# The last down block of each layer by seven quarter products, on one Trainium2 core

## The chip, the core and the metric

The kernel runs on one core of one Trainium2 chip. The core has a matrix engine (TensorE, PE in the profile), two elementwise engines (VectorE, DVE; ScalarE, ACT), a general engine (GpSimd, POOL) and a queue engine that issues most transfers (SyncE, SP). Each engine works through its own instructions in order; they wait for each other by semaphores. The results of matmuls land in eight PSUM banks of 128 rows by 512 float32.

The metric is the device time of one execution in microseconds (us), lower is better. Three runs of the kernel before took 1818.7, 1818.74 and 1818.12 us; the median is 1818.7 us.

## What is computed

A decoder trunk of two layers over 512 tokens of width 1024. Only the second half of a layer matters here, the MLP with its two norms:

```python
h2 = rmsnorm(x, pre_mlp_g)
ff = jnp.square(jax.nn.relu(h2 @ w_ff1)) @ w_ff2     # 1024 -> 4096 -> 1024
return x + rmsnorm(ff, post_mlp_g)
```

The output is the (1, 512, 1024) array after the second layer. After the first layer, x is normed again (`pre_mix_g`) and multiplied by the next input projection.

## The kernel before

**Precision.** Every float32 matmul is done as three: both operands are split into a high part (rounded) and a low part (the rest), and hi·hi + hi·lo + lo·hi are added in PSUM. A weight chunk of 128x1024 numbers is loaded by SP (`load`, L278), its high part made by ACT (L384, tile `wh`), its low part by DVE (L385, tile `wl`). `weights()` (L389) hands out the chunks in the fixed order of `chunk_order` (L58) and prepares four ahead (`LOOK = 4`, four `wh` and four `wl` buffers; six `wr` buffers for the raw loads).

**The MLP.** The hidden width 4096 is done in four stages `s` of 1024. Each stage has an up block (h2 times a 1024-wide part of `w_ff1`, relu, square) and a down block (the result times a 1024-row part of `w_ff2`), and the four down blocks are summed. The sums are held in SBUF in `acc[t][n]`, eight 128x512 tiles: token tile `t` of 0 to 3, output half `n` of 0 or 1.

**Up blocks.** `SEQ[s]` (L45) gives the order of the eight 128-wide units of a stage. A plain unit is 24 matmuls of 512 columns (`mm_a`, L396). A pair in brackets, such as `(0, 1)`, is done by seven products of four 128-row blocks instead of eight (Winograd's form of Strassen's scheme): 84 matmuls of 256 columns (`mm_h`, L482), with sums of weights by DVE (L343). Stage 0 is plain, stages 1 and 2 mixed, stage 3 all pairs.

**Down blocks.** Stages 0 to 2 use the same scheme over quarters (512x512 blocks of the 1024x1024 weights, two token halves): seven products P1 to P7, each `mm_c` (L466) with 24 matmuls of 512 columns: 2 chunks `j` by 2 token tiles `t` by 2 row blocks by 3. `seven` (L291) makes the seven right operands from loaded quarters with sums by DVE (L304, L309); `lefts` and `make_later` (L1542, L1557) make the left ones. The order is P1, P5, P6, P2, P7, P3, P4. Each finished quarter is added to `acc` by DVE out of PSUM (`into` L1413, L1614, L1617, L1627). P4 of a stage is cut in two around the first product of the next stage where that starts with a pair (`split4`, L1629).

**Stage 3 before** (L1636 to L1668) is plain in its down block: `acc[t][0]` is copied into PSUM by ACT and 96 matmuls are added to it (`mm_b4`, L448), then mean square and gain for that half; then the other half, token tile by token tile.

- Layer 0 uses `last_tiles` (L427): tile 0 (24 matmuls), tile 1 (24), then tiles 2 and 3 together (48) with the transposes of the finished tiles 0 and 1 between them (`norm_turn`, L554: eight transposes on PE, then split by ACT and DVE into the next layer's left operand). The next layer starts with tiles 0 and 1 (42 matmuls of 432 columns) while tiles 2 and 3 are normed, then turns those.
- Layer 1 does one tile after the other, and writes each out.

**The tail of a token tile** is `post_tiles` (L559): mean square by ACT (L520), times the gain by DVE (L575), a small add (L525), the power by POOL (L526), then two DVE instructions that scale and add x (L578, L579). With a next layer follow the mean square of the new x (ACT, twice), the power again, and two scalings by DVE (L535), which make what the transposes read. Within one call the order of DVE and ACT is written out by hand (`Order`, L179); in the other places a planner in the compiler sets each engine's order before the run, mostly by program order among what it thinks ready.

## Time and profile before

| | us |
|---|---|
| median of 3 runs | 1818.7 |
| the profiled execution's own time | 1816.19 |
| its span, from the first to the last instruction | 1814.5 |
| layer 0, stage 2: P1's first matmul to P4's first | 785.63 to 818.51 |
| layer 0, stage 3 to the next layer's first matmul | 818.51 to 909.72 |
| layer 1, stage 2: P1's first matmul to P4's first | 1684.91 to 1717.79 |
| layer 1, stage 3, to its last matmul | 1717.79 to 1807.04 |

How to read it: the first part of the page gives the busy time of each engine. Rows of the timeline give the start of an instruction, its duration, engine, line, and operands by the program's names; what stands in square brackets is idle time of that engine before it, with what ended it. Matmuls overlap: one of 512 columns is listed with 0.39 us, but the next one starts sooner, so what a row of matmuls costs is read from their starts. The table of windows gives the busy time of each engine in a stretch, with the number of instructions, the granted TensorE clock and the share and rate of the transfers.

### The profile page before, as it was taken

The page shows a single profiled execution, that of the slowest core. Times are in us where ns is not written, and L with a number is a line of the kernel's source. Part 1 is how long each engine was busy: PE and PEld are TensorE (multiplying, and loading weights), DVE is VectorE, ACT ScalarE, POOL GpSimd, SP SyncE. Part 2 cuts the span into 40 slices and gives each one's busy share as a digit, 9 for nine tenths or more (in the row PEclk, how much of TensorE's full clock was granted, in tenths as well). Part 3 has the DMA queues.
Part 4 walks back from the last instruction along what each step waited for, and adds up shares of the span by engine and source line. Part 5 has one row for each costly group of instructions (what it writes and reads, how often), then busy time and mean ns, then how long its engine had stood idle before and what let it go on. Part 6 is the DMA issues. An engine that isn't in the chain of part 4 may idle for free.

```text
span 1814.5 us, 28394 instructions
## 1 busy us (share of the span) xinstructions
PE 1794.6 (99%) x10252; PEld 1524.7 (84%) x10252; DVE 1375.1 (76%) x2590; ACT 1007.5 (56%) x2065; POOL 210.6 (12%) x386
## 2 busy tenths in 40 slices
PE   9999999999999999999999999999999999999998
PEld 8878878888788888989898887888877888889896
DVE  5499796887666878898556997968875669698973
ACT  6678742444434656566556877234443347566572
POOL 0322102221101000000013221022111010000000
PEclk9999999999999999999999999999999999999999
DMA  5633447655463254554445334585545533555551
GB/s 201 203 112 121 111 146 226 178 172 152 117 208 129 82 164 156 174 180 145 168 160 176 106 127 111 169 232 159 163 140 154 171 116 105 174 162 164 174 178 56
DMA packets 146431, 278.60 MB, mean 154 GB/s; under 512 B 33569, under 2 KB 66657, under 8 KB 146290
## 3 DMA queue, kind: packets, MB, share of 16 engines
q1 hardware_dynamic: 145778, 276.75, 49.2%
q8 instruction: 81, 1.33, 0.3%
q14 instruction: 60, 0.49, 0.1%
q0 software_dynamic: 512, 0.03, 0.0%
HBM read 239.38 MB, written 37.36 MB: 153 GB/s over the span
## 4 chain that ended last, share of the span: by engine, by line
PE 88%; DVE 4%; ACT 4%; DMA 2%; issue 1%; POOL 0%; SPq 0%; DVEq 0%; POOLq 0%; ACTq 0%
PE ps_b L459 3%; PE ps_b L461 3%; PE ps_b L463 3%; PE ps_f L400 2%; PE ps_f L401 2%; PE ps_f L402 2%; PE ps_us L400 2%; PE ps_ud L400 2%; PE ps_us L401 2%; PE ps_ud L401 2%; PE ps_ud L402 2%; PE ps_us L402 2%; PE ps_vp L400 2%; PE ps_vp L402 2%; PE ps_vp L401 1%; PE ps_qp L401 1%
## 5 line engine op out<-in xcount | busy, mean ns | idle before, releaser
L384 ACT CAST wh<-wr 128x1024 fp32r<-128x1024 f32 (+2 forms) x368 | 372.7, 1019 | 430.4 <-PE ps_us L401 60.2
L385 DVE TENSOR_TENSOR wl<-wr,wh 128x1024 fp32r<-128x1024 f32 (+2 forms) x368 | 434.9, 1189 | 183.8 <-ACT wh L384 180.2
L526 POOL TENSOR_TENSOR pr<-pq,pw 128x1 f32<-128x1 f32 x16 | 9.8, 615 | 790.1 <-DVE pq L525 790.1
L459 PE MATMUL ps_b<-wh,h_h 128*128 128x432 f32 (+1 forms) x192 | 71.1, 370 | 0.0
L461 PE MATMUL ps_b<-wl,h_h 128*128 128x432 f32 (+1 forms) x192 | 70.4, 367 | 0.0
L463 PE MATMUL ps_b<-wh,h_l 128*128 128x432 f32 (+1 forms) x192 | 70.3, 366 | 0.0
L400 PE MATMUL ps_f<-g_h,wh 128*128 128x512 f32 x160 | 62.4, 390 | 0.0
L401 PE MATMUL ps_f<-g_l,wh 128*128 128x512 f32 x160 | 62.4, 390 | 0.0
L402 PE MATMUL ps_f<-g_h,wl 128*128 128x512 f32 x160 | 62.2, 389 | 0.0
L401 PE MATMUL ps_qp<-h_l,wh 128*128 128x512 f32 x128 | 53.9, 421 | 0.0
L400 PE MATMUL ps_vp<-h_h,wh 128*128 128x512 f32 x128 | 53.7, 420 | 0.0
L402 PE MATMUL ps_vp<-h_h,wl 128*128 128x512 f32 x128 | 53.7, 419 | 0.0
L995 ACT ACTIVATE M<-M,nm 128x128 f32<-128x128 f32 x128 | 49.8, 391 | 5.9 <-DVE nm L990 5.8
L400 PE MATMUL ps_qp<-h_h,wh 128*128 128x512 f32 x128 | 51.8, 405 | 0.0
L343 DVE TENSOR_TENSOR wr<-wr 128x512 f32<-128x512 f32 x72 | 47.5, 685 | 5.5 <-DMA wr<-in_weights_dram 5.2
L400 PE MATMUL ps_kp<-h_h,wh 128*128 128x512 f32 x128 | 51.6, 403 | 0.0
L402 PE MATMUL ps_qp<-h_h,wl 128*128 128x512 f32 x128 | 51.4, 401 | 0.0
L401 PE MATMUL ps_vp<-h_l,wh 128*128 128x512 f32 x128 | 51.3, 401 | 0.0
L401 PE MATMUL ps_ga<-h_l,wh 128*128 128x512 f32 x128 | 51.0, 398 | 0.0
L400 PE MATMUL ps_gb<-h_h,wh 128*128 128x512 f32 x128 | 51.0, 398 | 0.0
L402 PE MATMUL ps_kp<-h_h,wl 128*128 128x512 f32 x128 | 50.9, 398 | 0.0
L402 PE MATMUL ps_ga<-h_h,wl 128*128 128x512 f32 x128 | 50.7, 396 | 0.0
(435 smaller groups left out, 5928.4 us busy)
## 6 DMA issues: line engine op xcount, KB each, us to landing
wr<-in_weights_dram SPq DMA_DIRECT2D x320, 512.0 KB, 3.6
wr<-in_weights_dram SPq DMA_DIRECT2D x24, 432.0 KB, 5.2
D<-dd SPq DMA_DIRECT2D x32, 256.0 KB, 2.7
xd<-xo SPq DMA_DIRECT2D x12, 512.0 KB, 3.0
xt<-xd SPq DMA_DIRECT2D x24, 256.0 KB, 4.5
D<-gd SPq DMA_DIRECT2D x16, 256.0 KB, 6.2
dd<-D SPq DMA_DIRECT2D x16, 256.0 KB, 5.2
kkd<-kk SPq DMA_DIRECT2D x16, 256.0 KB, 2.0
```

The lines of the kernel that those rows point to most:

```text
L343: tt(out=o_, in0=i0, in1=i1, op=ALU.add)
L384: nc.scalar.copy(wh[:, :w], wr[:, :w])
L385: sub(out=wl[:, :w], in0=wr[:, :w], in1=wh[:, :w].bitcast(F32), op=ALU.subtract)
L400: mm(ps, lhsT=wh[:, k, :], rhs=hi, start=k == 0, stop=False)
L401: mm(ps, lhsT=wh[:, k, :], rhs=lo, start=False, stop=False)
L402: mm(ps, lhsT=wl[:, k, :], rhs=hi, start=False, stop=k == KT - 1)
L459: mm(pss[t], lhsT=hi[:, tsl], rhs=wh[:, r, :], start=k == 0 and not onto, stop=False, skip_group_check=onto)
L461: mm(pss[t], lhsT=hi[:, tsl], rhs=wl[:, r, :], start=False, stop=False, skip_group_check=onto)
L463: mm(pss[t], lhsT=lo[:, tsl], rhs=wh[:, r, :], start=False, stop=k == KT - 1, skip_group_check=onto)
L526: ptt(out=r, in0=q1, in1=mhalf[:, 0:1], op=ALU.pow)
L995: act(out=M[:, j * P:(j + 1) * P], in_=M[:, j * P:(j + 1) * P], func=AF.Exp, bias=nm[:, j:j + 1], accum_out=den[:, j:j + 1])
```

## The change

The change makes stage 3 of each layer like stage 0: its up block is plain (`SEQ[3]` becomes `FF_ORDER`), and its down block is done by the seven quarter products. Three things differ from the other stages. The order of the products is P1, P5, P6, P2, P3, P7, P4, with the right operands made in that order. Sums that are held in `acc` are added by DVE into PSUM before the last product of a quarter (`pa`, `pv`, and `pw_` after P7), so that the finished numbers stand in PSUM. Token tiles 0 and 1 are finished after P3 and go through `post_tiles` together, tiles 2 and 3 after P4; there the half that is finished last is half 0 (`late = 0`). In layer 0 the transposes of tiles 0 and 1 stand behind the first and second half of P4. In layer 1 P4 is done for tile 2 and then for tile 3.

```diff
-SEQ = (FF_ORDER, (0, 1, (4, 5), (2, 3), 6, 7), ((0, 1), (4, 5), (2, 3), 6, 7), ((0, 1), (2, 3), (4, 5), (6, 7)))
+SEQ = (FF_ORDER, (0, 1, (4, 5), (2, 3), 6, 7), ((0, 1), (4, 5), (2, 3), 6, 7), FF_ORDER)
@@ chunk_order
             out.append(("up", l, s))
-            if s < 3:
-                out.append(("seven", "w_ff2", l, s * 1024))
-                continue
-            for n in range(2):
-                for j in range(4):
-                    b_in("w_ff2", s * 1024 + j * 256, n * 512, 512)
+            out.append(("seven", "w_ff2", l, s * 1024))
@@ seven
+        if r0 == 3072:
+            makes = makes[:4] + (makes[5], makes[4], makes[6])
@@ mm_c
-    def mm_c(pss, left, onto=False, js=range(2)):
+    def mm_c(pss, left, onto=False, js=range(2), ts_=range(2), ws=None):
         for j in js:
-            wh, wl = weights()
+            wh, wl = ws[j] if ws else weights()
             hi, lo = left[j]
-            for t in range(2):
+            for t in ts_:
@@ post_tiles: 512: and :512 become hb_ and ha, set by the new argument late
+        ha, hb_ = (slice((h_ % 2) * 512, (h_ % 2 + 1) * 512) for h_ in (late + 1, late))
@@ ff2_tail
+            late = 0 if tiles[0] > 1 else 1
+            a0 = [a[1 - late] for a in acc]
@@ the stages
-        for s in range(3):
+        for s in range(4):
...
-                make("P4", T[2], a22, -1.0)
+                make("P4", T[2], a22, -1.0 if s < 3 else 1.0)
...
             make_later("P3", T[1])
+            if s == 3:
+                break
@@ stage 3, in place of ff1, mm_b4, last_tiles and the loop over tiles
+        def early_half(t, n, src):
+            s0[t] = meansq(src, "pq0")
+            tt(out=acc[t][n], in0=src, in1=gb3[:, n * 512:(n + 1) * 512], op=ALU.mult)
+
+        for t in range(2):
+            tt(out=pa[t], in0=pa[t], in1=acc[t][0], op=ALU.add)
+            tt(out=pv[t], in0=pv[t], in1=acc[t][1], op=ALU.add)
         if l < depth - 1:
             nxt = pre_begin(l + 1)
             xs_next = []
+        mm_c(pa, left["P2"], True)
+        for t in range(2):
+            early_half(t, 0, pa[t])
+        mm_c(pv, left["P3"], True)
+        ff2_tail((0, 1), pv)
+        mm_c(pw_, left["P7"], True)
+        for t in range(2):
+            tt(out=acc[2 + t][1], in0=pw_[t], in1=acc[2 + t][1], op=ALU.add)
+            tt(out=pw_[t], in0=acc[2 + t][0], in1=pw_[t], op=ALU.subtract)
+        for t in range(2):
+            early_half(2 + t, 1, acc[2 + t][1])
+        if l < depth - 1:
             order = Order(nc.tensor)
             order.begin()
-            last_tiles(ws, h3, "ps_f2", ff2_tail, lambda t: norm_turn(xs_next[t], t, nxt[1]),
-                       [a[1] for a in acc])
+            for j in range(2):
+                mm_c(pw_, left["P4"], True, (j,))
+                norm_turn(xs_next[j], j, nxt[1])
+            ff2_tail((2, 3), pw_)
             hT = nxt
         else:
-            for t in range(NT):
-                ps = (PS if t % 2 else PZ)("ps_f2")
-                nc.scalar.copy(ps, acc[t][1])
-                mm_b(ps, ws, h3, t, onto=True)
-                ff2_tail((t,), [ps])
+            ws = [weights() for j in range(2)]
+            for t in range(2):
+                mm_c(pw_, left["P4"], True, ts_=(t,), ws=ws)
+                ff2_tail((2 + t,), pw_[t:])
```

## The prediction

> **What bounds the kernel now.** I read the page's busy times and its chain first, then the timeline of PE around both stages 3, then DVE's groups and timeline in stage 2, which already has the down block that stage 3 is to get.

> ```profile
> span 1814.5 us, 28394 instructions
> ...
> PE 1794.6 (99%) x10252; PEld 1524.7 (84%) x10252; DVE 1375.1 (76%) x2590; ACT 1007.5 (56%) x2065; POOL 210.6 (12%) x386
> ...
> PE 88%; DVE 4%; ACT 4%; DMA 2%; issue 1%; POOL 0%; SPq 0%; DVEq 0%; POOLq 0%; ACTq 0%
> ```

> PE is busy 99% of the span and 88% of the chain: a matmul less is time less, as long as nothing makes PE wait. The timeline of PE gives what a matmul costs and where the stages lie:

> ```profile
> 818.51 0.39 PE L475 MATMUL ps_pw<-wh,P_h 128*128 128x512 f32 x1
> ...
> 821.23 0.28 PE L487 MATMUL ps_a<-g_h,wh 128*128 128x256 f32 x1
> ...
> 822.67 0.40 PE L475 MATMUL ps_pw<-wh,P_h 128*128 128x512 f32 x1
> ...
> 864.83 0.40 PE L463 MATMUL ps_b<-wh,h_l 128*128 128x512 f32 x1
> ...
> 886.16 0.39 PE L420 MATMUL ps_f<-wh,h_h 128*128 128x512 f32 x1
> ...
> 909.72 0.35 PE L420 MATMUL ps_b<-wh,h_h 128*128 128x432 f32 x1
> ```

> From 818.51 to 821.23 stand 12 matmuls of 512 columns: 2.72/12 = 0.2267 us each. From 821.23 to 822.67 stand 12 of 256 columns: 1.44/12 = 0.120 us each. From 818.51 to 909.72 (91.21 us) stand 24 + 192 of the first kind, 336 of the second and 16 transposes (0.79 us per eight, first row of the fence on the transposes below): 5.44 + 43.53 + 40.32 + 1.58 = 90.9. So stage 3 has no gap worth the name, and PE bounds it alone.

> DVE is the engine to look at next. Its windows in stage 2, from P1's first matmul to P4's, in layer 0 and in layer 1:

> ```profile
> 785.63:818.51 32.88, 32.88 (x146) 27.21 (x145) 31.41 (x38) 19.20 (x26) 0.00 (x0) 1.00 0.50 160
> 1684.91:1717.79 32.88, 32.88 (x146) 27.21 (x145) 31.02 (x37) 19.30 (x26) 0.00 (x0) 1.00 0.52 160
> ```

> The third pair is DVE: 31.41 of 32.88 us, 96%. ACT (19.2) and the transfers (share 0.50) have room. The six products there run on a DVE that is nearly full. What it does, by groups, and its first and last steps:

> ```profile
> L385 DVE TENSOR_TENSOR wl<-wr,wh 128x1024 fp32r<-128x1024 f32 x11 | 13.2, 1222 | 2.0 <-ACT wh L384 2.0
> ...
> L304 DVE TENSOR_TENSOR wr<-wr 128x1024 f32<-128x1024 f32 x3 | 3.7, 1223 | 0.2 <-DMA wr<-in_weights_dram 0.2
> L309 DVE TENSOR_TENSOR wr<-wr 128x1024 f32<-128x1024 f32 x2 | 2.4, 1218 | 0.0
> ...
> L1417 DVE TENSOR_TENSOR acc<-ps_pa,acc 128x512 f32<-128x512 f32 x2 | 1.3, 684 | 0.0
> ...
> L1614 DVE TENSOR_TENSOR acc<-ps_pw,acc 128x512 f32<-128x512 f32 x2 | 1.3, 682 | 0.0
> ```

> ```profile
> 786.69 1.22 DVE L385 TENSOR_TENSOR wl<-wr,wh 128x1024 fp32r<-128x1024 f32 x1 [1.78 <-ACT wh L384]
> ...
> 813.39 1.28 DVE L1614 TENSOR_TENSOR acc<-ps_pw,acc 128x512 f32<-128x512 f32 x2
> ```

> DVE starts 1.06 us after P1's first matmul, since it could not work ahead (1.78 us idle: the fourth chunk waits for a buffer that the last up unit still reads), and has its list done at 818.33 (the first L1617, quoted under rival B), just before P4. So there is no spare DVE time in these six products.

> **The change, part by part.** *PE, up block:* 336 matmuls of 256 columns become 192 of 512: 192 x 0.2267 - 336 x 0.120 = 43.53 - 40.32 = +3.21 us per layer. *PE, down block:* 192 become 168: -24 x 0.2267 = -5.44. Net -2.23 per layer, **-4.5 us** in all. [...]

> *Transfers:* the down block loads 16 chunks in place of 8, on SP's queue, ahead of the next layer's. Stage 2 does just that at a share of 0.50, with 0.2 us of DVE waiting for a load; I take nothing. Were that cover gone, one late chunk would cost PE up to its 2.72 us. *ACT* loses the seeds of PSUM and is free. *Up block on DVE:* lighter than before (no L343), but as in stage 2 that buys nothing: the four buffers allow no more to be ahead at P1.

> *DVE in the down block,* until P4 may start. P4 accumulates onto `pw_`, which DVE must first rewrite in place after P7; that wait is new. Stage 2's list stands, minus the four additions out of PSUM behind P2 and P7 (L1417 on `pa`, L1614), plus: four additions into `pa` and `pv`, two multiplications by the gain behind P2, two in the tail of tiles 0 and 1 (L575), the sum for `acc[2][1]` and the rewriting of `pw_[0]`. That is 10 - 4 = 6 instructions of 128x512. An addition that writes PSUM does not occur before; nearest are 0.64 (the pair at 813.39) from below and 0.75 (L578) from above. At 0.62 to 0.64, six are 3.8 us. The tail of tiles 0 and 1 adds, by the groups of layer 0's end:

> ```profile
> L535 DVE SCALAR_TENSOR_TENSOR xs<-xo,nr,gb 128x512 f32<-128x512 f32 x8 | 5.7, 749 | 2.0 <-POOL nr L526 1.9
> L385 DVE TENSOR_TENSOR wl<-wr,wh 128x864 fp32r<-128x864 f32 (+1 forms) x5 | 5.4, 1089 | 1.3 <-ACT wh L384 1.2
> ...
> L578 DVE SCALAR_TENSOR_TENSOR xo<-acc,pr,xt 128x512 f32<-128x512 f32 x4 | 3.0, 749 | 1.4 <-POOL pr L526 1.4
> L579 DVE SCALAR_TENSOR_TENSOR xo<-xo,pr,xt 128x512 f32<-128x512 f32 x4 | 3.0, 746 | 0.0
> ...
> L525 DVE SCALAR_TENSOR_TENSOR pq<-pq,pq 128x1 f32<-128x1 f32 x4 | 0.6, 149 | 0.0
> ```

> four of L578/L579, 0.67 us each start to start, 2.7 us, and 0.2 for L525. Together 6.6 us more. All of it stands ahead of `pw_` in program order, and so do the last two chunks of weights (P4's own). Stage 2's list ended 32.7 us after P1 with 0.7 us idle in it and 0.23 us for a matmul (L1603) that stage 3 lacks. So `pw_[0]` is ready at 32.7 + 6.6 - 0.7 - 0.2 = 38.4 us; P4 is due at 6 x 5.44 = 32.65. **PE waits 5.8 us** in layer 1. Behind P4's first matmul on PE stands everything else; nothing fills the hole. `pw_[1]` follows 1.2 us later and is covered by the first matmuls of P4. Bounds: 3.1 if the planner puts the four L578/L579 behind `pw_`; 7.5 if DVE also waits a little for POOL's powers and ACT's squares.

> *Layer 0* has the same wait and more on DVE: one chunk of the next layer (1.0 us) and L525 (0.1) ahead of `pw_`, four of L535 (2.7 us) among it, and then the turned tiles, which the next layer's first matmuls need. The slack there, before:

> ```profile
> 917.87 1.04 PE L546 MATMUL ps_n<-ident,xs 128*128 128x128 f32 x8
> 918.66 0.44 PE L420 MATMUL ps_b<-wh,h_h 128*128 128x432 f32 x1
> ...
> 919.92 0.60 PE L546 MATMUL ps_n<-ident,xs 128*128 128x128 f32 x4
> 921.12 0.66 PE L546 MATMUL ps_n<-ident,xs 128*128 128x128 f32 x4 [0.60 <-DVE h_l L552]
> ```

> Already tile 3's transposes wait 0.60 us there. The new order moves eight transposes (0.79 us) between the last product and this point, which helps; a DVE about 2 us late takes it back. I take 5.8 + 1.1 + 0.3 = **7.2 us**; bounds 4.5 (as above, with the tail later) and 11 (all of L535 ahead of `pw_`, and the turn late by 2).

> *The end of layer 1:* the last two tiles end 12 matmuls (2.72 us) apart in place of 24. A tile's DVE work and its waits take:

> ```profile
> 1802.83 0.69 DVE L575 TENSOR_TENSOR xo<-ps_f,gb 128x512 f32<-128x512 f32 x1 [2.54 <-ACT jk L520]
> ...
> 1804.97 0.75 DVE L579 SCALAR_TENSOR_TENSOR xo<-xo,pr,xt 128x512 f32<-128x512 f32 x1
> ```

> 1804.97 + 0.75 - 1802.83 = 2.89 us, so tile 3 starts 0.2 us late at worst: +0.1.

> **Sum:** -4.5 + 5.8 + 7.2 + 0.1 = **+8.6 us**. The profiled execution's own time is 1816.19 us (1.7 around its span): 1824.8. The median of the runs is 2.5 above that execution, so the forecast is 1818.7 + 8.6 = **1827.3 us**.

> **The rivals.** *A, P4 does not wait (faster).* DVE's order, set before the run, would have to put the rewriting of `pw_` and P4's chunks first, and the rest of the tail into P4, and the idle microsecond at P1 would have to vanish. Then only PE's sum and the last tile are left: 1818.7 - 4.5 + 0.1 = 1814.3. For it: the six products of stage 2 never let PE wait, though DVE is 96% busy. Against it: 6.6 us more work do not fit into 1.5 us. It decides if DVE's added work before P4 is under 2 us. Chance 0.14.

> *B, half of it (no change).* The planner puts the four L578/L579 behind `pw_`: 3.1 and 4.5 us of waiting, -4.5 + 7.6 + 0.1 = +3.2, 1821.9. For it: in stage 2 it let two instructions of later work pass an addition out of PSUM:

> ```profile
> 818.33 0.68 DVE L1617 TENSOR_TENSOR acc<-ps_pv,acc 128x512 f32<-128x512 f32 x1
> 818.93 0.68 DVE L343 TENSOR_TENSOR wr<-wr 128x512 f32<-128x512 f32 x1
> 819.61 1.22 DVE L385 TENSOR_TENSOR wl<-wr,wh 128x1024 fp32r<-128x1024 f32 x1
> 820.76 0.68 DVE L1617 TENSOR_TENSOR acc<-ps_pv,acc 128x512 f32<-128x512 f32 x1
> ```

> Against it: there it was the addition that came late, which here is the rewriting of `pw_`. Chance 0.25, with all between A and the forecast.

> *C, the clock falls in the hole (slower still).* After the last matmul, whose issue ends at 1807.3, the windows show the granted clock:

> ```profile
> 1810.27:1811.27 1.00, 0.00 (x0) 0.00 (x0) 0.89 (x2) 0.00 (x0) 0.00 (x0) 0.81 0.00 0
> 1811.27:1812.27 1.00, 0.00 (x0) 0.00 (x0) 0.00 (x0) 0.00 (x0) 0.00 (x0) 0.50 0.92 342
> ```

> 0.81 is 0.62 us at 1.0 and 0.38 at 0.5: it halved at 1810.9, 3.6 us after. A wait of 5.8 us is longer. If the clock then stays low for as long as it took to fall, P4 loses some 1.8 us per layer (an estimate from this row), 1827.3 + 3.6 = 1830.9. [...] Against it: the wait may come in pieces. Chance 0.20.

> *D, the change takes effect in one layer only:* PE would then lose 144 + 24 instructions once, not twice (10252 to 9916), and half of the sum is left, 1823.0. The diff speaks against it. Chance 0.01.

> **How the numbers follow.** The forecast, 1824 to 1830, has 0.40. About 0.2% (3.6 us) is what a measurement of this kernel can tell from no change: 1815.1 to 1822.3 is "same". Faster is A: 0.14. Same is B: 0.25. Slower is the forecast, C and D: 0.61. Low end: between A and B, 1815.0, which leaves A out; high end: C with half of layer 0's way to its upper bound, 1833.0, which leaves out about 0.05.

> **What would show it.** PE has 9916 instructions and the up block of stage 3 takes 43.5 us without gaps. PE stands idle at P4's first matmul in both stages 3, released by DVE's rewriting of `pw_`, about 6 us. DVE is busy over 95% from P1 to there. Wrong would be: P4 without idle time ahead of it; DVE idle for more than 2 us between P1 and P4; a wait at P7's weights, which would put the loss one product earlier; a clock under 1.0 in P4 (C).

## The result, and the profile after

The changed kernel takes 1837.8 us (median of 4 runs, 1836.4 to 1838.3), the kernel before 1818.7 us (4 runs): ratio 1.0103, 95% interval 1.0085 to 1.0120. It is slower by 19.0 us, over twice the 8.6 forecast, and lies above the range (1815 to 1833). The profiled execution took 1838.32 us, 22.1 more than that of before.

The head of the page after, the busy times, the granted clock in 40 slices, and the chain by engine:

```profile
span 1836.6 us, 27720 instructions
...
PE 1796.9 (98%) x9916; PEld 1510.8 (82%) x9916; DVE 1398.1 (76%) x2606; ACT 1002.1 (55%) x2033; POOL 211.3 (12%) x386
...
PEclk9999999999999999999899999999999999999998
...
PE 83%; DVE 7%; ACT 4%; DMA 3%; issue 2%; POOL 1%; SPq 1%; DVEq 0%; POOLq 0%; ACTq 0%
```

PE has the 9916 instructions that its sum asked for, yet it is busy 2.3 us longer than before. The clock has an 8 in slice 20, where layer 0's stage 3 lies, and one at the end. The chain's DVE share went from 4% to 7%. What PE waits for (total, times, longest), the first two rows, which the kernel before does not have:

```profile
PE ps_pw L472 <- DVE ps_pw L1656: 11.1, 2, 8.5
PE ps_pa L472 <- DVE ps_pa L1643: 6.1, 2, 3.1
```

L1656 is the rewriting of `pw_`, on which P4 waits. L1643 is the addition into `pa`, on which P2 waits: a second wait in each layer, that the forecast did not have. PE's timeline at the ends of the blocks, layer 0 and then layer 1:

```profile
820.36 0.39 PE L472 MATMUL ps_pw<-wh,P_h 128*128 128x512 f32 x1
...
869.32 0.39 PE L472 MATMUL ps_pa<-wh,P_h 128*128 128x512 f32 x1
...
885.42 0.39 PE L476 MATMUL ps_py<-wh,P_l 128*128 128x512 f32 x1
888.87 0.47 PE L472 MATMUL ps_pa<-wh,P_h 128*128 128x512 f32 x1 [3.06 <-DVE ps_pa L1643]
...
896.03 0.39 PE L472 MATMUL ps_pv<-wh,P_h 128*128 128x512 f32 x1
...
906.68 0.39 PE L476 MATMUL ps_pw<-wh,P_l 128*128 128x512 f32 x1
915.57 0.76 PE L472 MATMUL ps_pw<-wh,P_h 128*128 128x512 f32 x1 [8.50 <-DVE ps_pw L1656]
...
920.83 0.28 PE L543 MATMUL ps_n<-ident,xs 128*128 128x128 f32 x1
...
925.25 0.44 PE L417 MATMUL ps_b<-wh,h_h 128*128 128x432 f32 x1
```

```profile
1733.26 0.39 PE L472 MATMUL ps_pw<-wh,P_h 128*128 128x512 f32 x1
...
1782.22 0.39 PE L472 MATMUL ps_pa<-wh,P_h 128*128 128x512 f32 x1
...
1798.32 0.39 PE L476 MATMUL ps_py<-wh,P_l 128*128 128x512 f32 x1
1801.77 0.76 PE L472 MATMUL ps_pa<-wh,P_h 128*128 128x512 f32 x1 [3.07 <-DVE ps_pa L1643]
...
1808.78 0.39 PE L472 MATMUL ps_pv<-wh,P_h 128*128 128x512 f32 x1
...
1819.43 0.39 PE L476 MATMUL ps_pw<-wh,P_l 128*128 128x512 f32 x1
1822.38 0.76 PE L472 MATMUL ps_pw<-wh,P_h 128*128 128x512 f32 x1 [2.56 <-DVE ps_pw L1656]
...
1829.10 0.39 PE L476 MATMUL ps_pw<-wh,P_l 128*128 128x512 f32 x1
```

A matmul of 512 columns takes 0.2267 us from start to start, so a product of 24 takes 5.44. What is more than that is lost:

| us | layer 0 | layer 1 |
|---|---|---|
| wait ahead of P2 | 888.87 - 885.65 = 3.22 | 1801.77 - 1798.55 = 3.22 |
| P2 itself, over 5.44 | 7.16: 1.72 | 7.01: 1.57 |
| wait ahead of P4 | 915.57 - 906.91 = 8.66 | 1822.38 - 1819.66 = 2.72 |
| P4, over 5.44 (layer 0: first half, over 2.72) | 5.26: 2.54 | 6.95: 1.51 |
| stage 3, before (quoted ahead) | 91.21 | 89.25 |
| stage 3, after | 925.25 - 820.36 = 104.89 | 1829.10 - 1733.26 = 95.84 |
| difference | +13.7 | +6.6 |

The losses are 16.1 and 9.0 us; with PE's -2.23 per layer they give +13.9 and +6.8, which is what the starts show within 0.2. The rest of the 22.1 us, 1.85, lies ahead of the first stage 3 (818.51 to 820.36), where both kernels run the same instructions: a difference between two executions.

Why P2 and P4 themselves are longer is shown by the windows around them. The column to read is the one behind POOL's, the granted clock:

```profile
890.00:891.00 1.00, 1.00 (x5) 0.77 (x4) 1.00 (x2) 0.00 (x0) 0.00 (x0) 0.56 0.20 82
891.00:892.00 1.00, 1.00 (x4) 0.81 (x3) 1.00 (x2) 0.00 (x0) 0.00 (x0) 0.50 0.00 0
...
893.00:894.00 1.00, 1.00 (x5) 0.75 (x4) 0.38 (x1) 0.00 (x0) 0.00 (x0) 0.74 0.73 66
910.00:911.00 1.00, 0.00 (x0) 0.00 (x0) 1.00 (x3) 1.00 (x2) 0.59 (x1) 0.80 0.82 287
...
920.00:921.00 1.00, 1.00 (x5) 0.70 (x4) 0.00 (x0) 0.00 (x0) 0.00 (x0) 0.58 0.66 232
1801.00:1802.00 1.00, 0.23 (x1) 0.26 (x2) 1.00 (x3) 0.00 (x0) 0.00 (x0) 0.74 0.95 344
```

0.56 is 0.12 us at full clock and 0.88 at half: half the clock from 890.12 to 893.52, and from 910.60 to 920.84. It begins within a wait or just after it and lasts into the product. The losses are added up along PE's time; that each comes back when its cause is removed does not follow (e1 and e4 below).

DVE's timeline in layer 0 shows what stands ahead of the two instructions that PE waits for:

```profile
886.24 1.28 DVE L1415 TENSOR_TENSOR acc<-ps_py,acc 128x512 f32<-128x512 f32 x2
...
888.03 0.69 DVE L1643 TENSOR_TENSOR ps_pa<-ps_pa,acc 128x512 f32<-128x512 f32 x1
...
895.59 0.69 DVE L1640 TENSOR_TENSOR acc<-ps_pa,gb 128x512 f32<-128x512 f32 x1 [2.21 <-ACT jk L517]
...
908.78 1.42 DVE L532 SCALAR_TENSOR_TENSOR xs<-xo,nr,gb 128x512 f32<-128x512 f32 x2 [0.44 <-POOL nr L523]
...
911.84 1.41 DVE L532 SCALAR_TENSOR_TENSOR xs<-xo,nr,gb 128x512 f32<-128x512 f32 x2 [0.44 <-POOL nr L523]
...
914.74 0.69 DVE L1656 TENSOR_TENSOR ps_pw<-acc,ps_pw 128x512 f32<-128x512 f32 x1
```

The addition into `pa` (L1643) needs only P1 and numbers that are held since stage 2, but it stands behind an addition that needs the end of P6 (L1415). The late P2 then makes DVE itself idle for 2.21 us (2.06 in layer 1), since the next in its queue is the multiplication of P2's sum by the gain (L1640), which the trace shows released by ACT's mean square of that sum. And in layer 0 all four scalings of the next norm (L532) stand ahead of `pw_`.

### The profile page after: what moved, and what is told of

The parts are those of the page before. It is cut to its first block, busy times and chain, and to the rows that moved or that the text cites. A ratio compares the mean times of both kernels' runs of the same rounds, so it can differ in the third digit from the quotient of the medians.

```text
span 1836.6 us, 27720 instructions
## 1 busy us (share of the span) xinstructions
PE 1796.9 (98%) x9916; PEld 1510.8 (82%) x9916; DVE 1398.1 (76%) x2606; ACT 1002.1 (55%) x2033; POOL 211.3 (12%) x386
## 3 DMA queue, kind: packets, MB, share of 16 engines
q8 instruction: 78, 1.28, 0.3%
## 4 chain that ended last, share of the span: by engine, by line
PE 83%; DVE 7%; ACT 4%; DMA 3%; issue 2%; POOL 1%; SPq 1%; DVEq 0%; POOLq 0%; ACTq 0%
PE ps_f L398 4%; PE ps_f L397 4%; PE ps_f L399 4%; PE ps_b L456 2%; PE ps_b L458 2%; PE ps_b L460 2%; PE ps_us L397 2%; PE ps_us L399 2%; PE ps_us L398 2%; PE ps_vp L397 2%; PE ps_vp L399 2%; PE ps_vp L398 1%; PE ps_pw L472 1%; PE ps_pa L472 1%; PE ps_ud L398 1%
## 5 line engine op out<-in xcount | busy, mean ns | idle before, releaser
L397 PE MATMUL ps_f<-g_h,wh 128*128 128x512 f32 x288 | 112.2, 390 | 0.0
L398 PE MATMUL ps_f<-g_l,wh 128*128 128x512 f32 x288 | 112.2, 390 | 0.0
L523 POOL TENSOR_TENSOR pr<-pq,pw 128x1 f32<-128x1 f32 x16 | 10.9, 680 | 814.0 <-DVE pq L522 813.7
L399 PEld LDWEIGHTS ps_f<-g_h,wl 128*128 128x128 f32 x288 | 54.1, 188 | 11.3
L397 PEld LDWEIGHTS ps_f<-g_h,wh 128*128 128x128 f32 x288 | 54.1, 188 | 10.9
L398 PEld LDWEIGHTS ps_f<-g_l,wh 128*128 128x128 f32 x288 | 54.1, 188 | 10.8
L472 PE MATMUL ps_pw<-wh,P_h 128*128 128x512 f32 x128 | 51.8, 404 | 11.1 <-DVE ps_pw L1656 11.1
L299 DVE TENSOR_TENSOR wr<-wr 128x1024 f32<-128x1024 f32 x48 | 58.5, 1220 | 1.2 <-DMA wr<-in_weights_dram 0.7
L472 PE MATMUL ps_pa<-wh,P_h 128*128 128x512 f32 x128 | 51.4, 402 | 6.1 <-DVE ps_pa L1643 6.1
L398 PE MATMUL ps_ud<-yT_l,wh 128*128 128x512 f32 x128 | 50.1, 391 | 2.5 <-DVE yT_l L498 2.5
L474 PE MATMUL ps_pw<-wl,P_h 128*128 128x512 f32 x128 | 51.3, 400 | 0.0
```

The lines of the kernel that those rows point to most:

```text
L299: tt(out=held[j], in0=held[j], in1=part(i, k, j), op=ALU.add)
L397: mm(ps, lhsT=wh[:, k, :], rhs=hi, start=k == 0, stop=False)
L398: mm(ps, lhsT=wh[:, k, :], rhs=lo, start=False, stop=False)
L399: mm(ps, lhsT=wl[:, k, :], rhs=hi, start=False, stop=k == KT - 1)
L472: mm(pss[t], lhsT=hi[:, c], rhs=wh[:, r, :], start=first, stop=False, skip_group_check=onto)
L474: mm(pss[t], lhsT=hi[:, c], rhs=wl[:, r, :], start=False, stop=False, skip_group_check=onto)
```

## The experiments

Four theories were tested. **Q**: PE waits because of the place of single instructions in DVE's queue. **W**: DVE's work between P1 and P4 is more than fits, wherever it stands. **C**: the half clock is a consequence of PE's waits. **S**: a helping engine slows DVE. All edits are to the changed kernel; medians of 4 runs or more, each beside the kernel before on the same chip (1817.7 to 1819.1 us).

### One place at a time: e1, e2, e3

```diff
 e1_pa_behind
-            tt(out=pa[t], in0=pa[t], in1=acc[t][0], op=ALU.add)
...
-            early_half(t, 0, pa[t])
+            into(t, 0, pa[t])
+            early_half(t, 0, acc[t][0])
 e2_tail_behind
-        ff2_tail((0, 1), pv)
         mm_c(pw_, left["P7"], True)
...
             tt(out=pw_[t], in0=acc[2 + t][0], in1=pw_[t], op=ALU.subtract)
+        ff2_tail((0, 1), pv)
```

> The held sums of acc[0][0] and acc[1][0] are not added into pa ahead of P2, but out of PSUM behind P2 (into), and mean square and gain read the sum from acc. DVE has the same number of instructions. Theory Q (PE waits for the place of one instruction in DVE's queue): P2's wait (3.2 us in each layer) and the half clock after it (1.7 and 1.6 us) go, P4's waits stay at 8.7 and 2.7 us: 1837.8 - 9.7 = 1828.1. Theory W (all of DVE's work ahead of pw_ is the bound, the place doesn't matter): P2's wait goes, but P4 waits as much longer as PE comes earlier, about 11 us in layer 0 and 5.5 in layer 1; only DVE's idle time behind the late P2 (2.2 and 2.1 us) and the half clock at P2 are gained: 1830 to 1833.

> The tail of tiles 0 and 1 stands behind the rewriting of pw_ in program order; no work is added or removed. Theory Q: P4's waits fall from 8.7 to about 1 us in layer 0 and from 2.7 to about 0 in layer 1, and the half clock in P4 (2.5 and 1.5 us) goes with them, about 14 us in all: 1824; P2's waits (3.2 us each) stay. Theory W: what waited at P4 waits behind it: the transposes of tile 0 and the next layer's first products stand idle for what P4 no longer waits, and the end of layer 1 comes later by the tail of two tiles (about 3 us): 1835 to 1838.

> Both edits of e1_pa_behind and e2_tail_behind. Theory Q: no wait is left at P2 and P4, and no half clock: the sum of both, 1837.8 - 9.7 - 14 = 1814, which is the time before with PE's sum (-4.5 us) and nothing else. Theory W: the waits come back at the transposes of tile 0 and in the first products of the next layer, and at the end of layer 1: 1825 to 1832.

Measured: e1 1833.0 us, e2 1831.4, e3 1828.7 (1.0061, 1.0046 to 1.0076). The waits of PE in e1, and then in e3:

```profile
PE ps_pw L472 <- DVE ps_pw L1656: 15.0, 2, 10.4
```

```profile
PE ps_n L543 <- DVE xs L532: 4.6, 1, 4.6
...
PE ps_pw L474 <- DVE wl L382: 2.9, 2, 1.9
...
PE ps_pw L472 <- DVE ps_pw L1655: 1.4, 2, 1.0
```

In e1 the wait ahead of P2 is gone, but those at P4 grew from 11.1 to 15.0. The gain is 4.7 us (4.4 in the stages 3 of the trace). P4 starts 43.70 us after P1 in layer 0 and 37.82 in layer 1, for 46.25 and 40.16: 2.6 and 2.3 us earlier, about DVE's idle time behind P2 (2.2 and 2.1). P2's half clock is gone too, but PE spends what that gains waiting at P4. The time lies at the edge of W's range. e2 lies between the two theories: the wait at P4 is nearly gone, in layer 0 4.8 us came back at the transposes of tile 0, and layer 1 ends 8.9 us behind its last matmul (span 1828.0, last matmul 1819.1) for 7.5. In e3 the products wait 1.4 us in all for an addition, and PE waits for weights (`wl`) and for the transposes instead; layer 1 ends 9.4 us behind its last matmul. Q's 1814 is missed by 15 us. So the place decides some 9 of the 19 us, and the rest moves on.

### The clock: e4

```diff
+        def keep_busy(ps, n):
+            for _ in range(n):
+                mm(ps, lhsT=zero_r, rhs=h2[0][0], start=False, stop=True, skip_group_check=True)
+        keep_busy(pw_[0], 14)
         mm_c(pa, left["P2"], True)
...
         mm_c(pw_, left["P7"], True)
+        keep_busy(pa[0], 12 if l == depth - 1 else 37)
```

`zero_r` is a tile of zeros.

> PE multiplies by a tile of zeros in the two waits (14 matmuls of 512 columns ahead of P2, 37 and 12 ahead of P4, added onto PSUM tiles that are there already), so that it isn't idle; DVE's list is that of the changed kernel. Theory C (half the clock is a consequence of PE's idle time): the granted clock stays 1.0 in P2 and P4, DVE's rewriting ends at the same times, and the 7.3 us that P2 and P4 lost are gained: 1830.5. Rival: the half clock has another cause (it falls at these times whatever PE does), or the zero matmuls make PE late by themselves: 1837 to 1841.

Measured: 1830.6 us, 7.2 less than the changed kernel (12.6 over the kernel before on its own chip, for 19.0). Two of the windows quoted above, in e4:

```profile
891.00:892.00 1.00, 1.00 (x6) 0.84 (x5) 1.00 (x1) 0.00 (x0) 0.00 (x0) 1.00 0.37 33
...
910.00:911.00 1.00, 1.00 (x6) 0.82 (x5) 0.88 (x2) 0.57 (x2) 0.42 (x1) 1.00 0.80 321
```

PE works on zeros where it waited, and the clock stays at 1.00 (0.50 and 0.80 above). C is shown: the half clock follows from PE's idle time. That the gain meets the 7.3 us of the table is in part luck. In the traces the stages 3 are 4.0 us shorter in layer 0 and 1.3 in layer 1; the other 2.6 us between the two executions lie where both run the same instructions. In layer 1 P2 lost nothing, yet P4 started no earlier, 40.27 us after P1 for 40.16:

```profile
1815.83 0.47 PE L474 MATMUL ps_pw<-wh,P_h 128*128 128x512 f32 x1 [1.38 <-DVE ps_pw L1669]
```

There the planner put one more lo part (1.2 us of DVE) ahead of `pw_`, and what PE gained in P2 became wait at P4, behind the zeros. So the clock is worth 5 to 7 us here.

### Less of PE's work ahead of the same down block: e6

```diff
-... ((0, 1), (4, 5), (2, 3), 6, 7), FF_ORDER)
+... ((0, 1), (4, 5), (2, 3), 6, 7), ((0, 1), (4, 5), (2, 3), (6, 7)))
```

In e6 and e7 the sum in `py` leaves out a part of -P1, in columns that the last pair's matmuls had not set, so their outputs are not the layer's; the instructions and their sizes are those of the full sum.

> The changed kernel with the up block of stage 3 left in pairs, 336 matmuls of 256 columns for 192 of 512; the last down block is the changed one. If PE's sum holds, each layer gains 3.2 us: 1837.8 - 6.4 = 1831.4, with the waits at P2 and P4 as they are. Rival: DVE also makes the sums of weights of the pairs and comes into the down block later, so that the waits at P2 and P4 grow by 1 to 3 us in each layer: 1833 to 1838.

Measured: 1837.7 us, no change, although PE's up block is 3.1 us shorter in layer 0 (from P4 of stage 2 to P1, 866.42 - 820.54 = 45.88, for 869.32 - 820.36 = 48.96) and 1.1 in layer 1, where PE waits 1.1 us for a lo part in it. The windows from P1's first matmul to P2's, in layer 0 of the changed kernel and then in both layers of e6; the third pair is DVE:

```profile
869.32:888.87 19.55, 16.48 (x73) 13.36 (x72) 18.49 (x25) 15.08 (x22) 0.00 (x0) 1.00 0.36 111
```

```profile
866.42:888.70 22.28, 17.05 (x76) 13.48 (x74) 22.28 (x30) 15.71 (x23) 0.00 (x0) 0.93 0.75 244
1778.14:1800.73 22.59, 17.05 (x75) 13.47 (x74) 22.59 (x31) 15.90 (x24) 0.00 (x0) 1.00 0.68 218
```

Counted from the stage's start, P2 starts 0.4 us earlier in layer 0 and 1.9 later in layer 1. In between DVE is busy 22.28 of 22.28 us, and 22.59 of 22.59 in layer 1, and the wait at P2 grew from 6.1 to 10.1 us in all. So what PE gained became wait, as W has it. But e6 does not hold DVE's work equal: DVE makes the sums for the pairs as well, and two sums of weights (L299) and a lo part or two, which the changed kernel has done before P1, are still to be made behind it (22.28 us of work for 18.49). Less of PE's work with no more for DVE was not tried.

### Less of DVE's work: e5, e7, e8, e10

```diff
 e5_pool_wl (with the edits of e3)
-            sub(out=wl[:, :w], in0=wr[:, :w], in1=wh[:, :w].bitcast(F32), op=ALU.subtract)
+            (ptt if src in by_pool else sub)(out=wl[:, :w], in0=wr[:, :w], ...)
 e8_dma_add, e10_dma_add3 (with the edits of e3; e10 without the two of both)
+        def onto(a, i, k, j):
+            pdma(a[:, :1024], wpk[index[(w, l, r0 + i * 512 + j * 256, k * 512, 512)], :, :1024],
+                 accum_op=ALU.add)
+            return a
...
         def add(i, k, j):
+            if r0 == 3072:
+                return onto(held[j], i, k, j)
             tt(out=held[j], in0=held[j], in1=part(i, k, j), op=ALU.add)
```

`by_pool` holds every second chunk of the last down block; `r0 == 3072` is that block; `both` makes the two sums for P7, in e8 the same way.

> e3_both, and POOL subtracts the low part of every second weight chunk of the last down block (7 of 14 in each layer, at an estimated 2.56 us each from L1191's 1279 ns for half the size) in place of DVE (1.22 us each, 8.5 us in each layer). Theory W (DVE's work is the bound): what is still lost in e3_both, counted from P1's first matmul, is 11.9 us in layer 0 and 2.6 us in layer 1; DVE is relieved of more than the change put on it, so most of it goes, 1815 to 1820. Rival S: the two engines slow each other, or POOL's subtractions come late themselves, and PE waits for them in place of DVE: 1828 or more.

> Both edits, e5_pool_wl and e6_pairs_up. Theory W: as e5_pool_wl, with the up block 3.2 us shorter in each layer: 1809 to 1814, faster than the kernel before. Rival: DVE, with the sums of weights of the pairs, is the bound again, and nothing is gained over e5_pool_wl.

Measured: e5 1839.8 us and e7 1841.4, 11 and 13 us over e3, whose edits both have: S. POOL's subtractions in e5, and DVE beside the long ones:

```profile
871.69 2.40 POOL L387 TENSOR_TENSOR wl<-wr,wh 128x1024 fp32r<-128x1024 f32 x1 [8.48 <-ACT wh L386]
879.36 9.34 POOL L387 TENSOR_TENSOR wl<-wr,wh 128x1024 fp32r<-128x1024 f32 x2 [5.26 <-ACT wh L386]
```

```profile
883.56 1.29 DVE L1420 TENSOR_TENSOR acc<-ps_pv,acc 128x512 f32<-128x512 f32 x2
884.75 4.49 DVE L503 TENSOR_TENSOR P_l<-S,P_h 128x512 fp32r<-128x512 f32 x2
```

Two subtractions of POOL take 9.34 us where one alone takes 2.40, and two of DVE with both operands in SBUF take 4.49 us, where two that read PSUM (L1420) take 1.29 at the same time. Not every such DVE instruction is slowed: one at 882.42 took its 1.23 us, and three of L503 from 880.62 on took 0.69 each. The rows show both engines slow in the same stretch, not why. So the help is looked for next in transfers, with no operand read by POOL:

> e3_both, and the eight sums of weights of the last down block (L299, L304: 1.22 us of DVE each, 9.8 us in each layer) are made by transfers that add into the loaded tile, issued by POOL, with no operand read by POOL itself. Theory W (DVE's work is the bound, and e5_pool_wl failed because POOL's reading slowed DVE): DVE's other instructions keep their times, and most of the 14.5 us that e3_both still loses between P1 and the next layer (11.9 in layer 0, 2.6 in layer 1) goes: 1815 to 1820. Rival: the adding transfers land late and PE waits for ACT's wh in place of DVE: over 1828.

> e8_dma_add, with the two sums for P7 made by DVE again (they came late there: their first load must land before the adding transfer can start, and DVE stood idle 3.8 and 2.8 us behind ACT's wh) and six by transfers, 7.3 us of DVE less in each layer than e3_both. Theory W: these idle times go, pw_ is ready some 4 us earlier than in e8_dma_add in each layer: 1819 to 1824. Rival (latency, not work, sets the end of P4's wait): no better than 1828.9.

Measured: e8 1828.9 us, no gain over e3, and e10 1821.1 us (10 runs; 1.0015, 1.0006 to 1.0024), 7.6 less than e3. DVE's timeline in e8 ahead of P7:

```profile
893.35 1.23 DVE L391 TENSOR_TENSOR wl<-wr,wh 128x1024 fp32r<-128x1024 f32 x1 [3.79 <-ACT wh L390]
```

The two sums for P7 by transfers came late (5.6 us from issue to landing), and DVE's queue stood behind them, 3.79 us and then 2.80; with these two back on DVE the idle time is gone. e10 takes 6 x 1.22 = 7.3 us of DVE's work away in each layer and is 7.6 us faster than e3 in all. What is left of e10's waits:

```profile
PE ps_n L550 <- DVE xs L539: 4.6, 1, 4.6
...
PE ps_pw L479 <- DVE ps_pw L1662: 2.5, 2, 1.6
```

4.6 us of it is layer 0's turn: tiles 0 and 1 are finished after P3, and their tail, norm and transposes have only P7 and P4 (10.9 us; tile 0 half of P4, 8.2) to be done in, in which DVE has P4's own additions and weights to make too.

### No product behind an addition: e13, e14; pairs again: e9

e13 and e14 put P4 into the free `pa` and add it behind; e13 has the adding transfers of e10, e14 has none.

```diff
-            tt(out=pw_[t], in0=acc[2 + t][0], in1=pw_[t], op=ALU.subtract)
+            tt(out=acc[2 + t][0], in0=acc[2 + t][0], in1=pw_[t], op=ALU.subtract)
...
-                mm_c(pw_, left["P4"], True, (j,))
+            mm_c(pa, left["P4"])
...
+                tt(out=acc[2 + t][0], in0=pa[t], in1=acc[2 + t][0], op=ALU.add)
 e9_pairs_dma (e8 and the pairs of e6)
             for t in range(2):
+                if isinstance(SEQ[s][-1], tuple):
+                    mm(py[t], lhsT=ones_r, rhs=h2[0][0], start=True, stop=True)
                 act(out=py[t], in_=pa[t], func=AF.Copy, scale=-1.0)
```

> The six adding transfers of e10_dma_add3, acc[0][0] and acc[1][0] added behind P2 as in e1_pa_behind, and P4 is no longer added onto the rewritten pw_: it goes into pa, which is free, and is added to the held sum by DVE after it (two instructions more in each layer); the transposes of tiles 0 and 1 stand behind the whole of P4. No product waits for an addition of DVE; only weights and the transposes can be late. Theory W with DVE relieved: all of the lost time but the last tile's extra addition (0.7 us) goes: 1814.3 + 1 to 4 for the transposes: 1815 to 1819. If something else than DVE's work and the rewriting holds PE up, it stays over 1824.

> e13_fresh without the adding transfers: DVE makes all sums of weights. Theory Q (only the place of the rewriting made PE wait): as e13_fresh, 1815 to 1819. Theory W (DVE's work is the bound): P4 does not wait for pw_, but PE waits for wl, for the transposes of tiles 0 and 1 and at the end of layer 1, for 5 us and more in all: 1822 to 1830.

Measured: e13 1823.8 us and e14 1832.2. e14 is far over what Q allows and 2 us over W's range, and e13 misses its 1815 to 1819 by 5. The transfers are worth 8.3 us between them, near the 7.6 from e3 to e10. With P4 free of DVE, e14 waits 4.7 us for a lo part (L549) at the transposes and 3.9 us for weights in P4: the wait follows the work, not the place. In e13 the transposes wait 4.6 and 1.9 us, and nothing else in the down block over 0.5; in both, layer 1 ends 2.4 us later behind its last matmul than before.

> e8_dma_add with the up block of stage 3 in pairs (3.2 us of PE less in each layer) and two matmuls that set py's banks before P6 (0.45 us more in each layer, and one in front of pw_). Theory W: 5 us below e8_dma_add, 1810 to 1815. If DVE, with the sums for the pairs, is the bound again, the same as e8_dma_add.

e9 missed both numbers: 1851.7 us. The adding transfers land late: PE waits 5.3 us at P5 and 2.7 at P6 for ACT's `wh`, which they feed. That the sums for the pairs hold the buffers for raw weights is likely but not shown; more buffers were not tried.

### Layer 1 alone: e15, e16

```diff
+def seq(l, s):
+    return LAST if (l, s) == (1, 3) else SEQ[s]
...
-        for s in range(4):
+        for s in range(4 if l == depth - 1 else 3):
```

> Layer 0 is that of the kernel before (pairs up, plain down block); layer 1 alone is changed, with the edits of e10_dma_add3. In e10_dma_add3 layer 1 lost 1.2 us of waits between P1 and its last matmul, layer 0 8.6 us, of which 4.6 at the transposes of tile 0. If PE's sum holds (-2.23 us in a layer) and layer 0's loss is the turn into the next layer, this kernel takes 1818.3 - 2.2 + 1.2 = 1817.3, 1816.5 to 1818.5. If PE's sum is not there, or the end of layer 1 is later by more than the waits show, 1819 to 1821.

> e15_layer1 with the up block of layer 1's stage 3 in pairs (3.2 us less of PE, 0.7 us more for three matmuls that set PSUM banks) and four adding transfers in place of six (those for P6 and P4). If DVE keeps up: 2.5 us below e15_layer1, 1814 to 1816. If the sums for the pairs fill DVE again, as in e6_pairs_up: no better than e15_layer1.

Measured: e15 1817.75 us beside 1817.73 (11 and 21 runs; 0.9996, 0.9987 to 1.0005), e16 1821.9 (1.0021, 1.0012 to 1.0030). PE in layer 1 of e15, from P4 of stage 2 to the last matmul, and the last DVE instruction:

```profile
1721.24 0.39 PE L489 MATMUL ps_pw<-wh,P_h 128*128 128x512 f32 x1
...
1803.96 0.47 PE L489 MATMUL ps_pw<-wh,P_h 128*128 128x512 f32 x1 [0.96 <-DVE ps_pw L1699]
...
1809.30 0.39 PE L493 MATMUL ps_pw<-wh,P_l 128*128 128x512 f32 x1
...
1813.78 0.75 DVE L594 SCALAR_TENSOR_TENSOR xo<-xo,pr,xt 128x512 f32<-128x512 f32 x1
```

Stage 3 takes 1809.30 - 1721.24 = 88.06 us for 89.25 before: -1.19, that is PE's -2.23 and the wait of 1.11 at P4 (1803.96 - 1802.85). The span ends 8.5 us behind the last matmul (1817.8 - 1809.3), for 7.46 before (1814.5 - 1807.04): the tail of tiles 0 and 1, put behind `pw_`, delays that of tiles 2 and 3 by 1.0. PE's sum is there, and is given back almost whole. In e16, with pairs, PE waits eight times in the down block, 3.8 us for DVE and 1.3 for ACT.

No version beats the kernel before; e15 equals it.

## Why the prediction was too low, step by step

The mechanism was right: PE waits for DVE, whose work ahead of P4 does not fit. Two steps of the sum put the time out of the range: the half clock behind the waits, which it had at nothing (7.3 us along PE's time), and layer 0's wait, which it had too small (7.2 us for 11.9). A third, that there is one wait, at P4, failed as well, but costs less: e1, without the wait at P2, is still 1833.0.

- **PE's sum, -4.5 us:** right. 9916 instructions, the up block without a gap, and e15 shows the -2.23 of one layer within 0.1. The end of layer 1 (+0.1) is right too: 7.50 us behind the last matmul, 7.46 before.
- **DVE is full in the six products:** right, and the heart of the matter; e10, and e13 beside e14, show it by taking work away. **That a lighter up block buys it nothing** holds against stage 2 (DVE idles ahead of its first lo part behind P1 there too, 1.78 us, here 2.35), but not against the pairs: e6, which has them, has 3.8 us more of DVE's work between P1 and P2 of layer 0.
- **The in-place addition, 0.62 to 0.75 us:** 0.69 (L1643), from start to start 0.60.
- **"All of it stands ahead of `pw_`", so one wait, at P4:** this step failed. The additions into `pa` and `pv` were counted as DVE's work, not as something that PE waits for, and P2 waits for L1643. Layer 1's waits together, 5.94 us, meet the 5.8 only by chance: DVE idled 2.06 us behind the late P2, and the last chunk's `wl` (1.14 us) stood behind `pw_`, not ahead.
- **Layer 0, 7.2 with an upper bound of 11:** 11.9 us of waits (3.22 + 8.66). The case that I held for the bound, all of the norm's scalings ahead of `pw_`, is the one that DVE's timeline shows.
- **Rival C, the clock, 0.20:** it came true and was mis-sized. The sum put it at nothing; it should have been a term of it: 3.1 us in layer 1 and 4.3 in layer 0, for 1.8 each. "The wait may come in pieces" was taken to speak against it, and pieces of 2.7 and 3.2 us were enough (in e3 one of 1.86).
- **The sum:** -4.5 + 9.0 + 16.1 + 0.1 = +20.7 in the profiled execution, for +8.6. Of the 12.1 between them, 7.3 are the clock along PE's time (e4 gave back 7.2 in its median, 5.3 in its trace), 4.7 layer 0's waits, and 0.1 layer 1's.
- **Rival A** would have needed DVE's added work to be under 2 us: e10, with 7.3 us less in each layer, more than the 6.6 that were added, is still 7 us above its 1814.3, most of it in layer 0, where the turn alone waits 4.6.
- **"Wrong would be DVE idle for more than 2 us":** it was, 2.21 and 2.06, as a consequence of the wait at P2 that was missed. For the same reason DVE was busy 90% and 91% from P1 to P4 (41.76 of 46.25 us, 36.70 of 40.16), not over 95%.

## What to carry to other kernels

Trading matmuls for elementwise work is a trade with the engine that has to take the work: look at its busy share in the very stretch, and for each instruction that a matmul will wait for, at what stands ahead of it in that engine's queue, not at the last of them alone. Price a wait of PE with the half clock behind it (here 1.5 to 2.5 us behind waits of 2.7 to 8.7), and where waits can't be avoided, matmuls by zero in them cost no time here and keep the clock (1.00 in both windows of e4, and 7.2 us less). Where the bound is work, moving an instruction moves the wait; only taking work away, by something beside which the full engine kept its times, helped (here transfers: in e8 DVE's low parts took 1.21 to 1.23 us beside them, and e10 is 7.6 us faster than e3; with POOL, in e5, two DVE subtractions took 4.49 us, for 1.28 in e8, and the time was 11 us over e3).

## What the runs showed of the hardware

- **The clock halved behind short waits.** In the changed kernel waits of 3.2 us (P2, layer 0) and 2.7 us (P4 of layer 1) were each followed by about 3.4 us at half clock (890.12 to 893.52 behind the first). Waits of 1.05 and 1.00 us in layer 1 of e3 cost no clock (1.00 from 1775.38 to 1816.10). The half clock from 910.60 to 920.84 lasted 10.24 us, three times 3.413, and the starts worked out from the windows, 890.12, 910.60 and 1801.48, lie 6.0 and 267.0 times 3.413 us apart. Windows are therefore laid on that grid here. Two pairs of neighbouring ones, of e3 and then of e2:

```profile
897.66:901.07 3.41, 1.55 (x7) 1.00 (x6) 2.90 (x3) 2.23 (x3) 0.00 (x0) 1.00 0.90 256
901.08:904.48 3.40, 3.40 (x10) 2.34 (x8) 3.40 (x5) 0.21 (x1) 0.00 (x0) 0.50 0.95 275
```

```profile
1795.17:1798.58 3.41, 1.57 (x7) 1.34 (x8) 3.41 (x7) 0.85 (x2) 0.00 (x0) 1.00 0.79 280
1798.59:1802.00 3.41, 3.41 (x17) 2.81 (x16) 2.93 (x4) 0.59 (x3) 0.00 (x0) 1.00 0.17 28
```
